# First half of the rows normalised, turned and multiplied in two quarters, with a new table of orders, in a float32 decoder block

## The chip, the cores and the metric

One core of a Trainium2 chip runs the whole kernel. The metric is the device time of one execution in microseconds (us), lower is better. Engines are named as the profile names them: PE multiplies, PEld loads its weights, DVE works elementwise, ACT does activations and casts, POOL is the second elementwise engine and also issues DMAs, SP issues DMAs only.

## The reference

```
h = rms_norm(x, norm_g)                          # x: 1024 rows x 1024
proj = h @ w_in                                  # u, g_rnn, q, k, v, g_attn, m_rnn, m_attn
u = causal_depthwise_conv(u)                     # width 4
y_rnn = rg_lru(u) * silu(g_rnn)                  # block-diagonal gates, linear recurrence over the rows
y_attn = sliding_window_attention_with_sinks(rope(q), rope(k), v) * silu(g_attn)   # 16 heads, 4 kv heads, window 128
merged = sigmoid(m_rnn) * (y_rnn @ w_rnn_out) + sigmoid(m_attn) * (y_attn @ w_attn_out)
out = rms_norm(x + merged @ w_o, final_norm_g)
```

All tensors are float32.

## The kernel before

**Products.** A float32 product is made of three matmuls: each operand is split into a high part (`h`, a cast by ACT) and a low part (`l`, what is left, a subtraction by DVE), and high·high, high·low and low·high are added up in PSUM. The wide projections run as *pairs* of output blocks: a pair and the two halves of the rows make a 2x2 block product, which `Pair.run` does with seven products instead of eight. Its right-hand operands are B11, B21, B22 and the combinations T1 to T4 of the transposed, normalised rows; its left-hand operands are the weight blocks A and their sums S1 to S4. Each is four tiles of 128x512 in two parts. B11 and B21 hold the first 512 rows, B12 and B22 the others.

**The opening.** Before any combination can exist, the rows have to come in. For each half of the rows (`hf`): the sum of squares of each block of 128 rows (`rstd_of`, on ACT or DVE), a scaling by DVE (L649 `xt<-xt,rs`), 32 transposes by PE (L656 `pt<-ident,xt`), and `cut_g`, which splits each of eight PSUM tiles into high (ACT, L438) and low (DVE, L439). So that PE has work meanwhile, two of the pairs that need no combination (`FIRST`, two output pairs of the merge gate) are multiplied plainly: `first_raw` loads their weights, `first_split` splits them into `dh` and `dl`, and `first_half(p, hf)` makes 2 outputs x 8 blocks x 3 matmuls of 512 columns (tile `fd`, L588 to L590). `F11` and `F21` keep the whole float32 rows of the first half for T1, T3 and T4; they are made by ACT again from PSUM (L673) or by POOL as the sum of both parts (L675).

**The order.** The program is recorded as a list of operations with costs, buffers and priorities (`Plan`), and a planner lays it out engine by engine. Each engine then runs its own list strictly in that order. What sets the list is the table `TUNE`: offsets to priorities (`prep`, `att`, `lru`, ...), limits of buffers by kind, and `orders`, the sequence of pairs (`ug`, `k`, `v`, `q`, `ga`, `ma`, `mr`, `zr`, `za`), of attention units (`a` with its key head and block) and of `s` entries. An `s` entry makes four sums ahead of time and parks them in DRAM: `s0` to `s7` of a pair's weights, `s8` to `s11` of `w_o`. The sums of `w_o` are read back only if `s8` is in the sequence, which it is in neither kernel.

Line numbers are those of the kernel before; in the changed one every line after the table stands 8 lower down, and those after the opening 36.

Of the kernel before, what the change touches and what calls it, by code (L numbers as in the profile page):

```python
# [17 lines left out]
S = 1024  # L18
D = 1024
P = 128  # L20
HF = 512
KT = D // P
# [38 lines left out]
    'val': 95,
    'gate': 951,
    'lru': -1407,
    'qk': -125,
    'comb': 348,
    'ztl': -10,
    'xof': 233,
    'gzr': 8,
    'gza': 42,
    'gwo': 14,  # L70
# [282 lines left out]
def hybrid_block_kernel(ctx: ExitStack, tc: tile.TileContext, x, wall, wo, bd, vec, gfin,  # L353
# [81 lines left out]
    def split(h, l, src, cols, reads, wh, wl, prio=0, psum=False, scale=None):  # L435

        if scale is not None:
            ACT(lambda e: e.activation(h(), src(), AF.Identity, scale=scale()), cols, reads, wh, prio, aps=1)  # L438
            DVE(lambda e: e.scalar_tensor_tensor(l(), src(), scale(), h().bitcast(F32), op0=MUL, op1=SUB), cols,  # L439
                list(reads) + list(wh), wl, prio, ptr=1)  # L440
            return
        ACT(lambda e: e.copy(h(), src()), cols, reads, wh, prio)  # L442
        (DVE if psum else EW)(lambda e: e.tensor_tensor(l(), src(), h().bitcast(F32), op=ALU.subtract), cols,  # L443
                              list(reads) + list(wh), wl, prio)
# [18 lines left out]
    def col(i):  # L463
        return vec_t.t[:, i : i + 1]
# [138 lines left out]
    HC["B12"] = [(buf("B12", dt=F32R, name="B12h"), buf("B12", dt=F32R, name="B12l")) for _ in range(4)]  # L603
    WD = {}

    def first_raw(p):
        for b, n in ((0, "A11"), (3, "A12"), (1, "A21"), (2, "A22")):
            raw = load("raw0", n)
            WD[p, n] = [raw]
            DMA(lambda raw=raw, b=b: raw.t, lambda b=b: wall[U_MR + p, b], 1 << 18, [], [raw])  # L610

    def first_split(p):
        for n in ("A11", "A12", "A21", "A22"):
            h, l = buf("wd", dt=F32R, name="dh"), buf("wd", dt=F32R, name="dl")
            split_buf(h, l, WD[p, n][0])
            WD[p, n] = (h, l)

    def first_half(p, hf):

        for q, names in enumerate((("A11", "A12"), ("A21", "A22"))):  # L620
            ps = bank("fd")
            for k in range(KT):
                h, l = WD[p, names[k // 4]]
                bh, bl = HC[("B11", "B21", "B12", "B22")[2 * hf + k // 4]][k % 4]
                w = slice(k % 4 * P, k % 4 * P + P)
                PE(lambda ps=ps, h=h, l=l, w=w, bh=bh, bl=bl, k=k: three(ps, h, l, w, bh, bl, k == 0, k == KT - 1), 3,
                   [h, l, bh, bl], [ps])
            gate_half("r", 2 * p + q, hf, ps)

    xs = []  # L630
    for s in range(NB):
        xs.append([slot("xt"), slot("xt")])
        for q in range(2):
            DMA(lambda s=s, q=q: xs[s][q].t, lambda s=s, q=q: x[s * P : (s + 1) * P, HALF[q]], 1 << 18, [], [xs[s][q]])
        if s == 0:
            DMA(lambda: vec_t.t, lambda: vec, 32768, [], [vec_t])
        if s == 3:
            first_raw(0)
    for p in FIRST[1:]:
        first_raw(p)  # L640
    F11, F21 = ([slot(n) for _ in range(4)] for n in ("F11", "F21"))
    for hf in range(2):
        pts = [bank("pt") for _ in range(KT)]
        for s4 in range(4):
            xh = xs[4 * hf + s4]
            rs = rstd_of(xh)
            for q in range(2):
                pl.op([("DVE", 395.0)], [xh[q], rs], [xh[q]], lambda e, q=q, xh=xh, rs=rs:
                      nc.vector.tensor_scalar(xh[q].t, xh[q].t, rs.t, None, op0=MUL), port=True)  # L649

        def cut_g(h, l, ps, k):
            split(lambda: h.t, lambda: l.t, lambda: ps.t, HF, [ps, vec_t], [h], [l], scale=lambda: col(V_G + k))

        def turn(s4, k, hf=hf, pts=pts):
            xh = xs[4 * hf + s4]
            PE(lambda: nc.tensor.transpose(  # L656
                pts[k].t[:, s4 * P : (s4 + 1) * P], xh[k // 4].t[:, (k % 4) * P : (k % 4 + 1) * P], ident),
               1, [xh[k // 4]], [pts[k]], 256)

        if hf == 0:  # L660
            for s4 in range(4):
                for k in range(KT):
                    turn(s4, k)
            for p in FIRST:
                first_split(p)
            for k in range(KT):
                h, l = HC["B11" if k < 4 else "B21"][k % 4]
                cut_g(h, l, pts[k], k)
                f = (F11 if k < 4 else F21)[k % 4]

                def whole(e, f=f, h=h, l=l, k=k, ps=pts[k]):
                    if e == "ACT":
                        nc.scalar.activation(f.t, ps.t, AF.Identity, scale=col(V_G + k))  # L673
                    else:
                        nc.gpsimd.tensor_tensor(f.t, h.t.bitcast(F32), l.t.bitcast(F32), op=ADD)  # L675
# [686 lines left out]
```

## Time and profile before

| | |
|---|---|
| median of 3 runs | 885.35 us (884.28 to 885.56) |
| the profiled execution, its own time | 885.57 us |
| its span in the trace | 883.8 us |
| busy: PE / DVE / ACT / POOL | 860.1 / 764.6 / 640.1 / 93.3 us |
| PE's first instruction | at 8.31 us |
| first product of the opening (`fd`) | at 17.78 us |
| first product on rows of the second half | at 48.41 us |

"Busy" is the time in which an engine has an instruction under way. The stages used below are the opening (0 to 48 us), the recurrent branch (48 to 315), attention (315 to 650), the two output projections (650 to 810), and the last projection with the final norm.

### The profile page before, as it was taken

How to read it: one execution, taken by the hardware profiler on the slowest of the kernel's cores; microseconds unless marked ns; L12 is line 12 of the kernel's file. 1: busy time of each engine (PE TensorE's matmuls, PEld its weight loads, DVE VectorE, ACT ScalarE, POOL GpSimd, SP SyncE). 2: the span in 40 equal slices, each digit the busy share in tenths (PEclk: the TensorE clock that was granted, in tenths of full speed). 3: DMA queues.
4: the chain of work that ended last, by engine and by line, in shares of the span. 5: the costliest groups of instructions: out<-in, count | busy, mean ns of one | idle time of the engine just before them, and what ended most of it. 6: DMA issues, size and time to landing. Idle time of an engine off the chain costs nothing.

```text
span 883.8 us, 13278 instructions
## 1 busy us (share of the span) xinstructions
PE 860.1 (97%) x4040; PEld 710.7 (80%) x4040; DVE 764.6 (87%) x1555; ACT 640.1 (72%) x1339; POOL 93.3 (11%) x161
## 2 busy tenths in 40 slices
PE   5899999999999999999999999999999999999996
PEld 4688877788878888888888888888888887888885
DVE  6998997889998888887887877868899999979968
ACT  7655758597986598988898899999884446343751
POOL 2101010100110011011001000001111121101030
PEclk9999999999999999999999999999999999999999
DMA  9538784611246745574843644444778898565155
GB/s 319 192 134 279 250 280 120 220 42 55 84 124 194 201 124 193 144 183 144 212 120 120 186 123 138 143 126 130 260 248 288 279 311 294 179 228 130 48 95 191
DMA packets 101000, 157.58 MB, mean 178 GB/s; under 512 B 12352, under 2 KB 41920, under 8 KB 100928
## 3 DMA queue, kind: packets, MB, share of 16 engines
q1 hardware_dynamic: 88160, 117.39, 41.4%
q0 software_dynamic: 12768, 39.33, 15.5%
q8 instruction: 32, 0.52, 0.3%
q14 instruction: 40, 0.33, 0.1%
HBM read 103.46 MB, written 53.22 MB: 177 GB/s over the span
## 4 chain that ended last, share of the span: by engine, by line
PE 58%; DVE 17%; ACT 6%; DMA 4%; issue 3%; DVEq 0%; SPq 0%; ACTq 0%
PE pair L531 15%; PE pair L532 15%; PE pair L533 15%; PE ps_s L922 3%; PE ptp L956 2%; DVE wl L443 2%; PE o L1233 2%; PE o L1232 2%; PE o L1231 2%; DVE c L450 1%; DVE S L450 1%; ACT sm L945 1%; PE po L969 1%; DVE cu L752 1%; PE po L970 1%
## 5 line engine op out<-in xcount | busy, mean ns | idle before, releaser
L428 POOL DMA_DIRECT2D A<-in_wall_dram x114 | 61.5, 540 | 591.1 <-PE pair L533 128.1
L442 ACT CAST wh<-S 128x512 fp32r<-128x512 f32 x128 | 78.4, 622 | 24.5 <-DVE S L450 18.9
L443 DVE TENSOR_TENSOR wl<-S,wh 128x512 fp32r<-128x512 f32 x128 | 87.1, 683 | 4.7 <-ACT wh L442 3.8
L443 DVE TENSOR_TENSOR wl<-A,wh 128x512 fp32r<-128x512 f32 x96 | 65.6, 684 | 10.0 <-ACT wh L442 9.7
L937 ACT ACTIVATE sm<-sm,nm 128x256 f32<-128x256 f32 (+1 forms) x128 | 62.2, 489 | 0.3 <-DVE nm L930 0.2
L442 ACT CAST wh<-A 128x512 fp32r<-128x512 f32 x96 | 59.4, 619 | 2.0 <-PE pair L533 1.0
L450 DVE TENSOR_TENSOR c<-pair,u 128x512 f32<-128x512 f32 x64 | 43.9, 686 | 17.4 <-ACT u L554 12.6
L930 DVE CUSTOM_DVE_ANT_0 sm<-ps_s,mask_t,sink_t 128x256 f32<-128x256 f32 (+1 forms) x128 | 53.9, 459 | 3.9 <-PE ps_s L922 3.8
L945 ACT ACTIVATE sm<-sm,dn 128x256 f32<-128x256 f32 (+1 forms) x128 | 53.6, 488 | 0.3 <-DVE dn L942 0.2
L531 PE MATMUL pair<-B11h,wh 128*128 128x512 f32 x128 | 51.6, 403 | 0.6 <-DVE B12l L439 0.6
L531 PE MATMUL pair<-T4h,wh 128*128 128x512 f32 x128 | 51.0, 398 | 0.5 <-ACT u L554 0.4
L531 PE MATMUL pair<-T1h,wh 128*128 128x512 f32 x128 | 51.3, 400 | 0.0
L531 PE MATMUL pair<-T2h,wh 128*128 128x512 f32 x128 | 51.2, 400 | 0.0
L531 PE MATMUL pair<-B21h,wh 128*128 128x512 f32 x128 | 51.1, 399 | 0.0
L531 PE MATMUL pair<-T3h,wh 128*128 128x512 f32 x128 | 50.4, 394 | 0.1
L532 PE MATMUL pair<-B22l,wh 128*128 128x512 f32 x128 | 49.9, 390 | 0.3 <-DVE B22l L443 0.3
L532 PE MATMUL pair<-T3l,wh 128*128 128x512 f32 x128 | 50.1, 391 | 0.1
L532 PE MATMUL pair<-T4l,wh 128*128 128x512 f32 x128 | 50.0, 391 | 0.1
L533 PE MATMUL pair<-B11h,wl 128*128 128x512 f32 x128 | 50.0, 391 | 0.0
L533 PE MATMUL pair<-T4h,wl 128*128 128x512 f32 x128 | 50.0, 390 | 0.0
L532 PE MATMUL pair<-B11l,wh 128*128 128x512 f32 x128 | 50.0, 390 | 0.0
L532 PE MATMUL pair<-T1l,wh 128*128 128x512 f32 x128 | 49.9, 390 | 0.0
(281 smaller groups left out, 2619.1 us busy)
## 6 DMA issues: line engine op xcount, KB each, us to landing
A<-in_wall_dram POOLq DMA_DIRECT2D x114, 256.0 KB, 3.4
qt<-st_q SPq DMA_DIRECT2D x32, 256.0 KB, 3.3
sr<-in_wall_dram SPq DMA_DIRECT2D x24, 256.0 KB, 4.6
sum<-S SPq DMA_DIRECT2D x24, 256.0 KB, 4.2
S<-sum POOLq DMA_DIRECT2D x24, 256.0 KB, 4.5
xt<-in_x_dram SPq DMA_DIRECT2D x16, 256.0 KB, 5.4
A<-in_wall_dram SPq DMA_DIRECT2D x16, 256.0 KB, 4.9
tm_r<-tm SPq DMA_DIRECT2D x16, 256.0 KB, 2.2
```

The source lines that it names most:

```text
L428: pl.op([("POOL", 1000.0)], reads, writes, lambda e: nc.gpsimd.dma_start(dst(), src()), prio, move=move)
L442: ACT(lambda e: e.copy(h(), src()), cols, reads, wh, prio)
L443: (DVE if psum else EW)(lambda e: e.tensor_tensor(l(), src(), h().bitcast(F32), op=ALU.subtract), cols, list(reads) + list(wh), wl, prio)
L450: (eng or EW)(lambda e: e.tensor_tensor(dst.t, a.t, b.t, op=op), HF, [a, b], [dst], prio)
L531: nc.tensor.matmul(ps.t, h.t[:, w], bh.t, start=start and k == 0, stop=False, **kw)
L532: nc.tensor.matmul(ps.t, h.t[:, w], bl.t, start=False, stop=False, **kw)
L533: nc.tensor.matmul(ps.t, l.t[:, w], bh.t, start=False, stop=k == 3, **kw)
L922: nc.tensor.matmul(ps.t[:, j, o0 : o0 + pw], qt.t[:, h, :], K[m, half].t[:, c0 : c0 + pw], start=m == 0, stop=m == 1)
L930: DVE(lambda v, ps=ps, j=j, h=h, s=s: v.tensor_tensor_reduce(s.t[:, j, :], ps.t[:, j, :], att["mask"].t[:, 256 - w : 256], scale=-0.125, s ...
L937: ACT(lambda e, h=h, s=s, j=j: e.activation(s.t[:, j, :], s.t[:, j, :], AF.Exp, scale=-1.0, bias=nm.t[:, h : h + 1], accum_out=dn.t[:, h : ...
L945: ACT(lambda e, h=h, s=s, j=j: e.activation(s.t[:, j, :], s.t[:, j, :], AF.Identity, scale=dn.t[:, h : h + 1]), w, [(s, j), dn], [(s, j)], ...
L956: PE(lambda pt=pt, h=h, b=b: nc.tensor.transpose(pt.t[:, h, :], sm[h // 2].t[:, h % 2, b * P : (b + 1) * P], ident), 1, [(sm[h // 2], h % ...
```

## The change

**Quarters.** For the first half of the rows, transposes, cuts and plain products are done in two quarters of 256 rows (`qq`): 16 transposes, eight cuts of 256 columns, then 96 matmuls of 256 columns per quarter. Two blocks `k` share a PSUM tile `pt`. Quarter 0 needs only the first two blocks of rows. The second half is done as before.

**F11 and F21** are no longer read from PSUM by ACT or added by POOL, but added from both parts after the second quarter (`EW`: DVE or POOL, as the planner puts it).

**Loads.** With `fwi` 2 the weights A11 and A12 of the first pair come ahead of row block 3, all others ahead of the second half of the rows.

**The table.** New numbers and another sequence of pairs, units and sums.

```diff
-    'S': 6,
+    'S': 4,
-    'B': 11,
+    'B': 13,
-    'prep': 270,
-    'att': 91,
+    'prep': 210,
+    'att': 117,
...
-    'orders': 'ug0 k0 ug7 v0 ug5 ug4 ug3 ug1 q0 q1 ug2 a00 ga0 ma2 a01 a02 a03 a10 a11 a04 a05 q3 a12 '
-              'a13 ga3 a14 q2 a15 s0 a06 s5 a07 s10 ug6 s3 ma1 mr3 a16 a20 a21 a17 s4 s6 a22 a23 a24 '
-              'ma0 ga2 a25 s1 a26 a30 a31 a32 a33 a34 ma3 a35 a36 a27 mr2 ga1 a37 zr0 zr1 zr2 zr3 za0 '
-              'za1 za2 za3',
+    'orders': 'ug0 ug3 k0 v0 ug5 s11 ug4 ug7 ug1 q0 q1 ug2 a00 s4 ma3 a01 a02 a03 a10 a11 ga2 a04 q3 '
+              'a12 a05 a13 ga1 ug6 a06 a14 s3 a15 s1 a07 q2 ga3 a16 ma2 a20 s9 a21 a22 a23 a17 a24 '
+              'mr3 a25 ma1 a30 a26 a31 a32 a33 a34 s0 a35 ma0 a36 a27 s5 ga0 mr2 a37 zr0 zr1 zr2 zr3 '
+              'za0 za1 za2 za3',
...
+    def first_quarter(p, qq):
+
+        for q, names in enumerate((("A11", "A12"), ("A21", "A22"))):
+            if qq == 0:
+                FD[p, q] = bank("fd")
+            ps = FD[p, q]
+            cs = slice(256 * qq, 256 * qq + 256)
+            for k in range(KT):
+                h, l = WD[p, names[k // 4]]
+                bh, bl = HC[("B11", "B21")[k // 4]][k % 4]
+
+                def go(ps=ps, h=h, l=l, w=slice(k % 4 * P, k % 4 * P + P), bh=bh, bl=bl, k=k):
+                    nc.tensor.matmul(ps.t[:, cs], h.t[:, w], bh.t[:, cs], start=k == 0, stop=False)
+                    nc.tensor.matmul(ps.t[:, cs], h.t[:, w], bl.t[:, cs], start=False, stop=False)
+                    nc.tensor.matmul(ps.t[:, cs], l.t[:, w], bh.t[:, cs], start=False, stop=k == KT - 1)
...
+            for qq in range(2):
                 for k in range(KT):
-                    turn(s4, k)
-            for p in FIRST:
-                first_split(p)
+                    for s4 in (2 * qq, 2 * qq + 1):
+                        xh, pt = xs[s4], pts[4 * qq + k // 2]
...
+                if qq == 0:
+                    first_split(0, 0)
+                for k in range(KT):
+                    h, l = HC["B11" if k < 4 else "B21"][k % 4]
+                    pt = pts[4 * qq + k // 2]
+                    cs = slice(256 * qq, 256 * qq + 256)
+                    split(lambda h=h, cs=cs: h.t[:, cs], lambda l=l, cs=cs: l.t[:, cs], lambda pt=pt, k=k: pt.t[:, k % 2, :], 256,
+                          [pt, vec_t], [(h, qq)], [(l, qq)], TUNE["cutp"], scale=lambda k=k: col(V_G + k))
+                if qq == 0:
+                    first_split(0, 1)
+                    for p in FIRST[1:]:
+                        first_split(p, 0)
+                        first_split(p, 1)
+                for p in FIRST:
+                    first_quarter(p, qq)
...
-                pl.op([("ACT", 569.0), ("POOL", 1245.0)], [h, l, pts[k], vec_t], [f], whole, port=True)
-            for p in FIRST:
-                first_half(p, 0)
+                EW(lambda e, f=f, h=h, l=l: e.tensor_tensor(f.t, h.t.bitcast(F32), l.t.bitcast(F32), op=ADD), HF, [h, l], [f])
```

**Where instructions went.** The program lists of both kernels, engine by engine, show it; a number after a name tells one buffer from another of the same name.

PE, around the first product, before: the last transposes of row block 3 (`xt_120`), then the first output `fd_321`.

```order
L656 MATMUL pt_196<-ident_69,xt_120 128x128
L656 MATMUL pt_198<-ident_69,xt_120 128x128
L656 MATMUL pt_202<-ident_69,xt_120 128x128
L588 MATMUL fd_321<-B11h_283,dh_206 128x512
L589 MATMUL fd_321<-B11l_295,dh_206 128x512
L590 MATMUL fd_321<-B11h_283,dl_231 128x512
```

PE, the same place now: `xt_104` and `xt_112` are row blocks 0 and 1, `xt_114` and `xt_116` block 2, `xt_122` block 3.

```order
L693 MATMUL pt_191<-ident_69,xt_112 128x128
L693 MATMUL pt_193<-ident_69,xt_112 128x128
L693 MATMUL pt_245<-ident_69,xt_114 128x128
L693 MATMUL pt_249<-ident_69,xt_114 128x128
L693 MATMUL pt_253<-ident_69,xt_116 128x128
L693 MATMUL pt_261<-ident_69,xt_116 128x128
L652 MATMUL fd_268<-B11h_227,dh_175 128x256
L653 MATMUL fd_268<-B11l_235,dh_175 128x256
L654 MATMUL fd_268<-B11h_227,dl_185 128x256
L652 MATMUL fd_268<-B11h_241,dh_175 128x256
L653 MATMUL fd_268<-B11l_259,dh_175 128x256
L654 MATMUL fd_268<-B11h_241,dl_185 128x256
```

The first product moved ahead of the transposes of row block 3; most of the second quarter's transposes now stand behind all 96 matmuls of the first.

DVE, between the first cuts, before (`dl` weights' low parts, L577 sums of squares of the second half's rows):

```order
L443 TENSOR_TENSOR dl_264<-A21_129,dh_253 128x512
L577 ISA junk_277,ss_260<-xt_144 128x512
L577 ISA ss_260 128x1
L443 TENSOR_TENSOR dl_286<-A22_135,dh_271 128x512
L439 SCALAR_TENSOR_TENSOR B11l_295<-pt_181,vec_t_106,B11h_283 128x512
L581 TENSOR_TENSOR ss_260<-ss_260 128x1
L577 ISA junk_302,ss_291<-xt_152 128x512
L577 ISA ss_291 128x1
L439 SCALAR_TENSOR_TENSOR B11l_311<-pt_183,vec_t_106,B11h_297 128x512
```

DVE, now, the first quarter's cuts (256 columns):

```order
L447 SCALAR_TENSOR_TENSOR B11l_235<-pt_180,vec_t_106,B11h_227 128x256
L451 TENSOR_TENSOR dl_243<-A21_129,dh_233 128x512
L592 RECIPROCAL rs_257<-sd_239 128x1
L447 SCALAR_TENSOR_TENSOR B11l_259<-pt_180,vec_t_106,B11h_241 128x256
L677 TENSOR_SCALAR xt_122<-xt_122,rs_257 128x512
L677 TENSOR_SCALAR xt_124<-xt_124,rs_257 128x512
L447 SCALAR_TENSOR_TENSOR B11l_275<-pt_182,vec_t_106,B11h_263 128x256
L447 SCALAR_TENSOR_TENSOR B11l_284<-pt_182,vec_t_106,B11h_277 128x256
L447 SCALAR_TENSOR_TENSOR B21l_291<-pt_191,vec_t_106,B21h_286 128x256
```

The first cut now stands ahead of the scaling of row block 3 and of four of the weights' low parts. From that cut to the first one of the second quarter DVE's list holds 8 cuts, 6 `dl`, one `wl`, three `S`, 10 scalings, 2 sums of squares and 15 tiny operations.

POOL, before, the sums that made five of the eight F tiles:

```order
L675 TENSOR_TENSOR F11_307<-B11h_283,B11l_295 128x512
L675 TENSOR_TENSOR F11_319<-B11h_297,B11l_311 128x512
L675 TENSOR_TENSOR F11_337<-B11h_313,B11l_327 128x512
L675 TENSOR_TENSOR F21_381<-B21h_353,B21l_367 128x512
L675 TENSOR_TENSOR F21_402<-B21h_385,B21l_393 128x512
```

DVE, now, behind the last S of the opening: the second quarter's last cuts, and all eight F tiles.

```order
L447 SCALAR_TENSOR_TENSOR B21l_331<-pt_261,vec_t_106,B21h_319 128x256
L715 TENSOR_TENSOR F11_540<-B11h_227,B11l_235 128x512
L715 TENSOR_TENSOR F11_545<-B11h_241,B11l_259 128x512
L715 TENSOR_TENSOR F11_553<-B11h_263,B11l_275 128x512
L715 TENSOR_TENSOR F11_561<-B11h_277,B11l_284 128x512
L715 TENSOR_TENSOR F21_568<-B21h_286,B21l_291 128x512
L715 TENSOR_TENSOR F21_577<-B21h_293,B21l_302 128x512
L715 TENSOR_TENSOR F21_585<-B21h_304,B21l_314 128x512
L715 TENSOR_TENSOR F21_592<-B21h_319,B21l_331 128x512
L447 SCALAR_TENSOR_TENSOR B12l_602<-pt_510,vec_t_106,B12h_527 128x512
L725 SCALAR_TENSOR_TENSOR T1_611<-pt_510,vec_t_106,F11_540 128x512
```

The F tiles left POOL and ACT, and DVE makes them between the second quarter and the first tile of the second half.

Over the whole program ACT's table loads go from 51 to 44, PE's matmuls from 4040 to 4136, the weights' parked sums from six sets to five, and the sets of `w_o` sums from one to two.

More of the change, by code (lines that the diff above doesn't have):

```diff
@@ L36 @@
     'pen': 99999,
-    'zy': 5,
-    'zg': 3,
+    'zy': 7,
+    'zg': 2,
     'raw': 4,
     'raws': 10,
-    'S': 6,
+    'S': 4,
     'wc': 11,
-    'B': 11,
-    'psw': 58,
+    'B': 13,
+    'psw': 82,
     'psk': 1,
@@ L47 @@
     'ld': 14,
-    'lds': 21,
+    'lds': 20,
     'kv': 8,
-    'kvs': 3,
+    'kvs': 0,
     'qt': 3,
-    'qts': 5,
-    'P': 16,
+    'qts': 3,
+    'P': 14,
     'AO': 22,
@@ L56 @@
     'xo': 24,
-    'lru0': -135,
-    'xos': 10,
-    'prep': 270,
-    'att': 91,
[L61 to L70, printed above, removed]
+    'lru0': -78,
+    'xos': 8,
+    'prep': 210,
+    'att': 117,
+    'val': 92,
+    'gate': 545,
+    'lru': -1714,
+    'qk': -43,
+    'comb': 775,
+    'ztl': -377,
+    'xof': 500,
+    'gzr': 9,
+    'gza': 38,
+    'gwo': 21,
     'gxo': 3,
@@ L75 @@
     'sil': 100,
+    'cutp': 0,
+    'fsp': 0,
+    'fwi': 2,
     'sump': 200,
@@ L83 @@
     'mgd': 1,
[4 rows of a table removed]
-}
[4 rows of a table added]
+}
+FW = ({1: [(0, 0)], 3: [(0, 1), (1, 0)], 5: [(1, 1)]}, {1: [(0, 0)], 2: [(0, 1)], 3: [(1, 0), (1, 1)]},
+      {2: [(0, 0)], 3: [(0, 1), (1, 0), (1, 1)]}, {3: [(0, 0)], 4: [(0, 1), (1, 0)], 5: [(1, 1)]},
+      {3: [(0, 0), (0, 1), (1, 0), (1, 1)]}, {1: [(0, 0)], 3: [(0, 1)], 4: [(1, 0)], 5: [(1, 1)]})
 V_CW, V_CB, V_BA, V_BX, V_LAM, V_G = 0, 32, 40, 48, 56, 64
@@ L604, in hybrid_block_kernel, with first_raw @@
     WD = {}
-    def first_raw(p):
-        for b, n in ((0, "A11"), (3, "A12"), (1, "A21"), (2, "A22")):
+    def first_raw(p, part):
+        for b, n in ((0, "A11"), (3, "A12"), (1, "A21"), (2, "A22"))[2 * part : 2 * part + 2]:
             raw = load("raw0", n)
@@ L610, in first_raw, with first_split @@
             DMA(lambda raw=raw, b=b: raw.t, lambda b=b: wall[U_MR + p, b], 1 << 18, [], [raw])
-    def first_split(p):
-        for n in ("A11", "A12", "A21", "A22"):
+    def first_split(p, part):
+        for n in (("A11", "A12"), ("A21", "A22"))[part]:
             h, l = buf("wd", dt=F32R, name="dh"), buf("wd", dt=F32R, name="dl")
-            split_buf(h, l, WD[p, n][0])
+            split_buf(h, l, WD[p, n][0], TUNE["fsp"])
             WD[p, n] = (h, l)
@@ L628, in first_half @@
             gate_half("r", 2 * p + q, hf, ps)
+    FD = {}
+    def first_quarter(p, qq):
[11 more added lines that the diff above has]
+                    nc.tensor.matmul(ps.t[:, cs], l.t[:, w], bh.t[:, cs], start=False, stop=k == KT - 1)
+                PE(go, 3, [h, l, (bh, qq), (bl, qq)], [ps], 256)
+            if qq:
+                gate_half("r", 2 * p + q, 0, ps)
     xs = []
@@ L636, in hybrid_block_kernel @@
             DMA(lambda: vec_t.t, lambda: vec, 32768, [], [vec_t])
[L637 to L640, printed above, removed]
+        for p, part in FW[TUNE["fwi"]].get(s, ()):
+            first_raw(p, part)
     F11, F21 = ([slot(n) for _ in range(4)] for n in ("F11", "F21"))
     for hf in range(2):
-        pts = [bank("pt") for _ in range(KT)]
+        pts = [bank("pt") for _ in range(KT)] if hf else [bank("pt", [P, 2, 256]) for _ in range(KT)]
         for s4 in range(4):
@@ L660, in hybrid_block_kernel @@
         if hf == 0:
-            for s4 in range(4):
+            for qq in range(2):
                 for k in range(KT):
-                    turn(s4, k)
-            for p in FIRST:
-                first_split(p)
+                    for s4 in (2 * qq, 2 * qq + 1):
+                        xh, pt = xs[s4], pts[4 * qq + k // 2]
+                        PE(lambda s4=s4, k=k, xh=xh, pt=pt: nc.tensor.transpose(
+                            pt.t[:, k % 2, (s4 % 2) * P : (s4 % 2 + 1) * P], xh[k // 4].t[:, (k % 4) * P : (k % 4 + 1) * P], ident),
+                           1, [xh[k // 4]], [pt], 256)
+                if qq == 0:
[13 more added lines that the diff above has]
+                    first_quarter(p, qq)
             for k in range(KT):
                 h, l = HC["B11" if k < 4 else "B21"][k % 4]
-                cut_g(h, l, pts[k], k)
+                pl.op([("SP", 0)], [(h, 0), (h, 1), (l, 0), (l, 1)], [h, l], lambda e: None)
                 f = (F11 if k < 4 else F21)[k % 4]
[L671 to L675, printed above, removed]
-                pl.op([("ACT", 569.0), ("POOL", 1245.0)], [h, l, pts[k], vec_t], [f], whole, port=True)
-            for p in FIRST:
-                first_half(p, 0)
+                EW(lambda e, f=f, h=h, l=l: e.tensor_tensor(f.t, h.t.bitcast(F32), l.t.bitcast(F32), op=ADD), HF, [h, l], [f])
         else:
```

## The prediction

> **What bounds the kernel now.** The page first: busy time of the engines, and the chain of work that ended last.
>
> ```profile
> PE 860.1 (97%) x4040; PEld 710.7 (80%) x4040; DVE 764.6 (87%) x1555; ACT 640.1 (72%) x1339; POOL 93.3 (11%) x161
> ...
> PE 58%; DVE 17%; ACT 6%; DMA 4%; issue 3%; DVEq 0%; SPq 0%; ACTq 0%
> ```
>
> PE is busy for 97% of the span and carries 58% of the chain. Where its idle 23.7 us lie, the table by stage says (stretch, its length, then busy us of PE, PEld, DVE, ACT, POOL):
>
> ```profile
> 0.00:48.00 48.00, 34.45 (x162) 28.07 (x163) 38.98 (x109) 35.05 (x75) 8.42 (x11) 1.00 0.76 262
> 48.00:315.00 267.00, 265.84 (x1173) 217.55 (x1172) 243.03 (x401) 188.13 (x312) 23.85 (x44) 1.00 0.51 162
> 315.00:650.00 335.00, 334.49 (x1718) 281.00 (x1718) 271.10 (x685) 303.31 (x736) 30.64 (x57) 1.00 0.55 163
> 650.00:810.00 160.00, 159.61 (x705) 130.63 (x704) 149.08 (x245) 77.41 (x147) 22.53 (x40) 1.00 0.74 246
> 810.00:853.00 43.00, 42.88 (x189) 34.89 (x188) 40.24 (x67) 28.79 (x56) 6.78 (x8) 1.00 0.37 73
> 853.00:884.00 31.00, 22.79 (x101) 18.55 (x99) 22.20 (x53) 7.38 (x21) 1.08 (x2) 0.94 0.48 154
> ```
>
> 13.55 us lie in the opening and 8.2 in the final norm's tail. Between 48 and 853 us, the whole of pairs and attention, PE idles 1.16 + 0.51 + 0.39 + 0.12 = 2.2 us. So a new order of pairs can win about 2 us at most; it can lose more. The opening is the place to look, in PE's waits and then in its timeline (start, length, instruction, idle time before it):
>
> ```profile
> PE pt L656 <- DVE xt L649: 9.0, 2, 8.3
> PE fd L588 <- DVE B11l L439: 1.5, 1, 1.5
> PE fd L589 <- DVE B21l L439: 1.2, 1, 1.2
> PE fd L589 <- DVE B11l L439: 1.2, 1, 1.2
> PE pair L531 <- DVE B12l L439: 0.6, 1, 0.6
> ```
>
> ```profile
> 8.31 3.65 PE L656 MATMUL pt<-ident,xt 128*128 128x128 f32 x16 [8.31 <-DVE xt L649]
> 12.65 3.68 PE L656 MATMUL pt<-ident,xt 128*128 128x128 f32 x16 [0.69 <-DVE xt L649]
> 17.78 0.50 PE L588 MATMUL fd<-B11h,dh 128*128 128x512 f32 x1 [1.45 <-DVE B11l L439]
> ...
> 42.95 0.39 PE L589 MATMUL fd<-B21l,dh 128*128 128x512 f32 x1
> 43.18 0.40 PE L590 MATMUL fd<-B21h,dl 128*128 128x512 f32 x1
> 43.42 3.65 PE L656 MATMUL pt<-ident,xt 128*128 128x128 f32 x32
> 47.66 0.47 PE L531 MATMUL pair<-B11h,wh 128*128 128x512 f32 x1 [0.58 <-DVE B12l L439]
> ```
>
> Every wait names DVE. Matmuls of 512 columns start 0.227 us apart (42.95 to 43.18 is one step), so the 96 of the first half are 21.8 us of work; they took 17.78 to 43.42, that is 25.6. The mark for the sum is 47.66 us: there all of the first half is multiplied, the 32 transposes of the second are done, and PE idles next to nothing for 800 us.
>
> **The change, part by part.** Prices of the new forms, from the nearest rows. A matmul of 256 columns and a DVE cut of 256 columns both stand elsewhere in this trace:
>
> ```profile
> 336.62 1.12 PE L922 MATMUL ps_s<-K,qt 128*128 128x256 f32 x8
> 337.61 0.48 PE L922 MATMUL ps_s<-K,qt 128*128 128x256 f32 x2
> ...
> 160.94 2.07 DVE L439 SCALAR_TENSOR_TENSOR vst<-pv,vst 128x256 fp32r<-128x256 f32 x6
> ...
> L438 ACT ACTIVATE vst<-pv 128x256 fp32r<-128x256 f32 x8 | 2.5, 387 | 2.4 <-PE pv L866 2.2
> ...
> L439 DVE SCALAR_TENSOR_TENSOR vst<-pv,vst 128x256 fp32r<-128x256 f32 x8 | 2.8, 412 | 0.0
> ```
>
> Eight such matmuls take 337.61 - 336.62 = 0.99 us, 0.124 each, so a quarter's 96 take 11.9 and both 23.8, 2.0 more than before. A DVE cut lasts 0.41 us and repeats every (2.07 - 0.41) / 5 = 0.33; one of ACT lasts 0.39.
>
> *Start.* What ACT does before its first cut stays nearly the same: seven sums of squares, two casts of weights, three roots. Before, this ended with the second cast:
>
> ```profile
> 12.49 0.60 ACT L442 CAST dh<-A 128x512 fp32r<-128x512 f32 x1
> 13.11 1.28 ACT L716 ACT_TABLE_LOAD   x1
> ```
>
> So the first cut can start at 13.1 us; with 0.39 on ACT and 0.41 on DVE the first product comes at about 14.0, 3.8 us earlier than 17.78. The table load and two casts that stood ahead of it are moved behind it.
>
> *The first quarter.* PE's own work is 11.9 us plus 14 transposes, which at full pace (3.65 us for 32) are 1.6: it could be through at 27.5. DVE can't feed the second quarter by then. From its first cut at 13.5 to the second quarter's, its list (in the order) has 8 cuts x 0.33, 10 subtractions or sums, 10 scalings, 2 sums of squares and 15 tiny operations. Their repeat times:
>
> ```profile
> 56.59 1.89 DVE L450 TENSOR_TENSOR T<-T,F 128x512 f32<-128x512 f32 x3
> ...
> 33.30 2.45 DVE L649 TENSOR_SCALAR xt<-xt,rs 128x512 f32<-128x512 f32 x6
> ...
> L577 DVE CUSTOM_DVE_ANT_0 junk<-xt 128x512 f32<-128x512 f32 x4 | 2.7, 686 | 1.0 <-DMA xt<-in_x_dram 1.0
> ```
>
> That is 0.60, 0.40 and 0.69, and 0.1 for a tiny one: 2.6 + 6.0 + 4.0 + 1.4 + 1.5 = 15.5 us, so 29.0 is the floor. I take 31.0, because ACT and DVE also hand PSUM tiles to and fro, as here, where ACT waited until DVE had read the same tile:
>
> ```profile
> 23.95 0.69 ACT L673 ACTIVATE F<-pt,vec_t 128x512 f32<-128x512 f32 x1 [1.34 <-DVE B11l L439]
> ```
>
> In the first quarter two cuts share a tile, eight such turns; a quarter of a microsecond each is my estimate. The second quarter's first product then comes at 31.3. PE's 3 us of spare time ahead of it cost nothing, because DVE would not let it go on earlier.
>
> *The second quarter and the mark.* Its cuts come every 0.36 to 0.39 us, its products use up 0.37 per cut and output and there are four outputs, so PE runs through: 31.3 + 11.9 = 43.2. Four of the second half's transposes are already done; 28 more are 3.2 us, five of them between products. PE is at the mark at 46.4, against 47.66: **1.2 us won**. The ends: with DVE at its floor 29.0 it is 3.2; with DVE 2 us later than I take it, a loss of 0.8.
>
> *F tiles.* DVE gets 8 x 0.60 = 4.8 us. It loses what POOL's sums did to it; while they ran, tiny DVE operations of 0.16 us took up to 1.28:
>
> ```profile
> 17.80 4.75 POOL L675 TENSOR_TENSOR F<-B11h,B11l 128x512 f32<-128x512 f32 x3 [16.49 <-DVE ss L581]
> ...
> 21.43 1.16 DVE L726 TENSOR_SCALAR ab<-vec_t 128x8 f32<-128x8 f32 x1
> ...
> 27.73 1.28 DVE L723 TENSOR_TENSOR acc<-acc,z 128x8 f32<-128x8 f32 x1
> ```
>
> The cover for the rest is DVE's lead. Before, its last T1 part started here:
>
> ```profile
> 69.23 0.68 DVE L443 TENSOR_TENSOR T1l<-T,T1h 128x512 fp32r<-128x512 f32 x1
> ```
>
> PE needs it after 117 matmuls from the mark (96 plain ones, 12 of A11 x B11, 9 of T1): 47.66 + 26.6 = 74.2, a lead of 4.3 us. After: second cuts to 34.2, F to 39.0, then by the order ten larger operations (6.7 us with the tiny ones between), 14 of 0.66 and 24 of 0.60 to about 69.8; PE needs it at 46.4 + 26.6 = 73.0. The lead is 3.2 and holds. Cost nothing; without that lead up to 4.8.
>
> *Loads.* The second half's rows go behind four more weights on SP, 4 x 256 KB; at 390 GB/s in this stretch that is 2.7 us.
>
> ```profile
> 10.00:15.00 5.00, 4.31 (x21) 3.90 (x20) 3.38 (x11) 4.97 (x13) 0.00 (x0) 1.00 1.05 396
> 15.00:20.00 5.00, 3.41 (x15) 2.35 (x14) 4.97 (x13) 5.00 (x14) 2.19 (x2) 1.00 1.05 386
> ...
> 15.02 0.63 ACT L575 ACTIVATE junk<-xt 128x512 f32<-128x512 f32 x1
> ```
>
> ACT squared the first of these rows at 15.0 before, so it lands by 17.7 now; by the order ACT asks for it seven cuts and two casts after 13.1, at 17.0 or, with the turns, 18.7. Hidden, or late by 0.7 on an engine that waits for DVE there.
>
> *The rest of the table.* One more set of dead `w_o` sums and one pair whose S are made in place: DVE +4 x 0.60 = 2.4 us, covered by its 24 idle us between 48 and 315; POOL's queue gets three loads fewer. ACT drops seven table loads of 1.28, 9 us, and in attention it is busy 303.3 of 335, so some of PE's 2.2 us should go; I take 1.0, with ends of 2.2 won and 2.2 lost (its idle time doubled). The tail has the same list on PE; nothing there.
>
> **Sum.** 1.2 + 1.0 = 2.2 us: span 881.6, own time 885.57 - 2.2 = 883.4, and since the profiled execution is 0.2 above the median, 883.2 on the runs' scale. 0.2% or 1.8 us is about what a measurement here can tell from no change.
>
> **Rivals.** *(a) No change:* the opening's gain is given back, because DVE is late with a T tile or the second half's cuts. For it: DVE's 4.97 of 5.00 us in the row from 15 to 20. Against: the 3.2 us of lead. If the 1.2 goes, 884.4; with the 1.0 too, 885.4.
>
> *(b) The array stays at half pace in the thin first quarter: slower.* The first 32 transposes took 3.65 us per 16, the later ones 3.65 for 32, though the granted clock reads 1.00 in both stretches. If PE, fed now in drops, stays at half pace over all 96 products, they take 23.8 instead of 11.9 us: 14.0 + 23.8 + 1.6 + 0.9 for the cuts = 40.3 instead of 31.3, so 9 us later than in the sum: 892. Its 3 us of spare time hide the first 24 half-paced products at 0.124 each; beyond 42 the whole gain is gone, beyond 56 it is measurably slower. Against it: at 17.78, after 1.45 us idle, products ran at once at full pace.
> The Trainium skill (TensorE: Matmul & The Clock Gate, The HAM clock gate) says the array starts at half clock and gets the full one after about 3.4 us of sustained activity, in a window that runs freely. By an estimate from that page, with PE fed steadily from 15.4 us, at most some 30 products are half-paced, 6 beyond what is hidden: 0.7 us, 883.9 instead of 883.2. The half pace agrees with the trace; the granted clock in it does not show it.
>
> *(c) Weight loads set the pace of short matmuls.* PEld's 710.7 us over 4040 are 0.176 each, more than 0.124; then the second quarter takes 5.0 us longer, 888.2. Against: the L922 rows, one load each, ran at 0.124.
>
> *(d) The new order stalls in the middle: slower.* A pair whose weights or combinations come late stops PE for 0.6 us, as the last of the waits above did. With the opening's 1.2 kept, five such stops make 885.35 - 1.2 + 3.0 = 887.2, the point from which it is measurably slower; seven make 888.4. Against: 2.2 us in all 800 now, with the same limits of work per engine; for it: 15 of 32 pairs change places.
>
> **Chances.** The sum, with opening and middle near the values taken, 0.50 (0.40 of it faster, 0.10 same); opening at DVE's floor, 880 to 882, 0.17; (a) 0.18; (b) 0.05; (c) 0.03; (d) 0.07, all three slower. Faster 0.57, same 0.28, slower 0.15. The low end is 885.35 - 3.2 - 2.2 = 880.0; the high end takes in (a) and half of (d), 886.5.
>
> **What would show it.** Right: first `fd` near 14, second quarter's first near 31, the mark near 46.4, POOL without sums, PE idle under 2.2 us from the mark to 853. Wrong: products 0.2 us apart in the first quarter (b, c); DVE idle before B11l, waiting for ACT (my two microseconds too small); PE waits on T tiles between 60 and 80 us (a), or on `u`, `c`, `pw` behind 100 (d).

## The result, and the profile after

The changed kernel takes 891.74 us (median of 6 runs, 889.87 to 893.17), the kernel before 885.45 us in runs beside it (6 runs, 884.28 to 886.91). The ratio is 1.007 with a 95% interval of 1.0056 to 1.0085: **slower by 0.7%**, where 883.2 us was forecast. The profiled execution took 891.28 us, its span is 889.5 us. From the page of the changed kernel, busy time and the chain that ended last:

```profile
PE 862.8 (97%) x4136; PEld 717.1 (81%) x4136; DVE 768.7 (86%) x1573; ACT 634.5 (71%) x1339; POOL 83.7 (9%) x153
...
PE 67%; DVE 15%; ACT 9%; DMA 4%; issue 4%; SPq 1%; DVEq 0%; ACTq 0%
```

PE's busy time grew by 2.7 us, ACT's and POOL's fell, and PE still sets the time. The changed kernel's table by stage (stretch, length, busy us of PE, PEld, DVE, ACT, POOL, then granted clock, DMA share, GB/s) says where PE is idle now:

```profile
0.00:48.00 48.00, 35.77 (x262) 34.26 (x263) 38.95 (x106) 33.47 (x80) 0.70 (x6) 0.96 0.69 242
48.00:315.00 267.00, 266.08 (x1184) 218.23 (x1183) 245.95 (x428) 190.30 (x313) 23.80 (x44) 1.00 0.54 167
315.00:650.00 335.00, 330.96 (x1678) 276.73 (x1677) 264.97 (x661) 292.89 (x718) 30.52 (x57) 0.99 0.54 157
650.00:810.00 160.00, 158.48 (x704) 129.22 (x703) 151.72 (x256) 79.29 (x150) 19.13 (x35) 1.00 0.74 253
810.00:853.00 43.00, 43.00 (x191) 35.42 (x191) 42.93 (x72) 29.20 (x56) 6.08 (x7) 1.00 0.27 45
```

From 48 to 853 us PE idles 0.92 + 4.04 + 1.52 + 0 = 6.5 us, three times the 2.2 of before, and in the attention stage the granted clock is no longer 1.00. PE's waits in the changed kernel name the places:

```profile
PE pt L693 <- DVE xt L677: 8.7, 1, 8.7
PE ps_s L958 <- DMA K<-st_k: 2.6, 1, 2.6
...
PE pair L540 <- DVE T3l L451: 1.2, 2, 1.1
...
PE pair L539 <- ACT u L555: 1.0, 2, 0.7
```

The second row is new: in all of the kernel before PE never waited for K. PE's timeline there and in the opening:

```profile
8.72 4.57 PE L693 MATMUL pt<-ident,xt 128*128 128x128 f32 x20 [8.72 <-DVE xt L677]
14.53 0.39 PE L652 MATMUL fd<-B11h,dh 128*128 128x256 f32 x1 [1.24 <-DVE B11l L447]
...
16.83 0.55 PE L652 MATMUL fd<-B11h,dh 128*128 128x256 f32 x1 [1.11 <-DVE B11l L447]
...
31.91 0.36 PE L652 MATMUL fd<-B11h,dh 128*128 128x256 f32 x1
...
43.51 2.89 PE L684 MATMUL pt<-ident,xt 128*128 128x128 f32 x25
46.15 0.48 PE L596 MATMUL fd<-B12h,dh 128*128 128x512 f32 x1
...
354.98 0.22 PE L958 MATMUL ps_s<-K,qt 128*128 128x128 f32 x1
357.80 3.40 PE L958 MATMUL ps_s<-K,qt 128*128 128x128 f32 x15 [2.60 <-DMA K<-st_k]
```

The opening went as forecast: first product at 14.53, the second quarter's first at 31.9, its last just ahead of 43.5. At 46.15 three of the 64 transposes are still to come, so the mark (first half multiplied, second half transposed) is 46.15 + 3 x 0.11 = 46.5. The last two rows are the loss: PE stands for 2.6 us, and then 15 small matmuls take 3.40 us, 0.21 each, where the same form ran at 0.11. The granted clock says why (same columns as above, stretches of the opening and of the stop):

```profile
16.60:20.00 3.40, 3.17 (x15) 3.20 (x16) 2.83 (x7) 2.89 (x8) 0.00 (x0) 0.50 1.05 387
...
354.50:357.90 3.40, 0.80 (x5) 0.51 (x4) 2.89 (x5) 2.71 (x5) 0.54 (x1) 1.00 0.97 224
357.90:361.30 3.40, 3.40 (x16) 3.40 (x17) 2.47 (x13) 3.11 (x12) 0.00 (x0) 0.51 1.06 376
```

Behind the stop the array ran at half clock for 3.4 us. Stop and half pace together cost some 4.4 us: the excess of PE's start-to-start times over full pace, summed over 340 to 400 us, is 7.4 us against 3.0 before. SP's timeline in the changed kernel shows who was late:

```profile
347.15 0.32 SPq L434 DMA_DIRECT2D yr_dr<-tg  x1
348.15 0.32 SPq L434 DMA_DIRECT2D sg_dr<-tga  x1
350.60 0.32 SPq L434 DMA_DIRECT2D yr_dr<-tg  x1
351.01 2.46 SPq L434 DMA_DIRECT2D K<-st_k  x4
```

The four loads of key head 1's last two K tiles need nothing that was late, but SP issues in the order of its list, and there they stand behind two stores of `tg`. The second `tg` product is the last step of DVE's chain for the recurrence (DVE's timeline):

```profile
348.56 1.28 DVE L821 TENSOR_TENSOR_SCAN hs<-r,hs,i 128x512 f32<-128x512 f32 x1
349.88 0.69 DVE L458 TENSOR_TENSOR tg<-tg,hs 128x512 f32<-128x512 f32 x1
```

### The profile page after: what moved, and what is told of

Its sections match the earlier page's. It is cut to its first block, busy times and chain, and to the rows that moved or that the text cites. A ratio compares the mean times of both kernels' runs of the same rounds, so it can differ in the third digit from the quotient of the medians.

```text
span 889.5 us, 13510 instructions
## 1 busy us (share of the span) xinstructions
PE 862.8 (97%) x4136; PEld 717.1 (81%) x4136; DVE 768.7 (86%) x1573; ACT 634.5 (71%) x1339; POOL 83.7 (9%) x153
## 4 chain that ended last, share of the span: by engine, by line
PE 67%; DVE 15%; ACT 9%; DMA 4%; issue 4%; SPq 1%; DVEq 0%; ACTq 0%
PE pair L539 16%; PE pair L540 16%; PE pair L541 16%; PE ps_s L958 2%; PE o L1269 2%; PE o L1268 2%; PE o L1267 2%; DVE wl L451 2%; ACT sm L973 2%; ACT sm L981 2%; PE ptp L992 2%; DVE c L458 1%; DVE S L458 1%; DVE cu L788 1%; DVE hs L821 1%
## 5 line engine op out<-in xcount | busy, mean ns | idle before, releaser
L539 PE MATMUL pair<-B22h,wh 128*128 128x512 f32 x128 | 50.0, 391 | 0.3 <-DVE c L458 0.3
L540 PE MATMUL pair<-B21l,wh 128*128 128x512 f32 x128 | 50.1, 392 | 0.1
L541 PE MATMUL pair<-T2h,wl 128*128 128x512 f32 x128 | 50.0, 391 | 0.0
L541 PE MATMUL pair<-T3h,wl 128*128 128x512 f32 x128 | 50.0, 391 | 0.0
```

Of the source, the lines that this page charges most:

```text
L539: nc.tensor.matmul(ps.t, h.t[:, w], bh.t, start=start and k == 0, stop=False, **kw)
L540: nc.tensor.matmul(ps.t, h.t[:, w], bl.t, start=False, stop=False, **kw)
L541: nc.tensor.matmul(ps.t, l.t[:, w], bh.t, start=False, stop=k == 3, **kw)
```

## The experiments

The theory: the new table (numbers and order of pairs) made the loss, as single stops of PE, the one for K first. The rivals: the quarters themselves made the later stages late (F tiles on DVE); or the loss is no sum of places but PE's normal state under another list. Each group of runs had the kernel before beside it; it took 885.55, 886.16 and 885.52 us there.

| run | median, us | ratio to before (95%) |
|---|---|---|
| the change | 891.74 | 1.0070 (1.0056 to 1.0085) |
| quarters_oldtable | 886.73 | 1.0020 (1.0008 to 1.0032) |
| halves_newtable | 890.00 | 1.0061 (1.0049 to 1.0073) |
| k_first | 888.91 | 1.0046 (1.0034 to 1.0058) |
| quarters_oldorders | 900.43 | 1.0174 (1.0159 to 1.0188) |
| quarters_oldnumbers | 903.78 | 1.0202 (1.0182 to 1.0222) |
| filled_pause | 894.41 | 1.0098 (1.0083 to 1.0113) |
| filled_at_355 | 890.99 | 1.0058 (1.0045 to 1.0072) |
| k_first_tz | 886.07 | 1.0001 (0.9991 to 1.0011) |
| quarters_oldtable_fix | 887.52 | 1.0013 (1.0003 to 1.0024) |
| mended | 886.34 | 1.0010 (1.0001 to 1.0019) |

**The change in two halves.** In *quarters_oldtable* the code is the changed one and the table that of before; in *halves_newtable* the code is that of before and the table the new one.

```diff
 # quarters_oldtable, against the changed kernel (all numbers of the table, and the orders)
-    'S': 4,
+    'S': 6,
...
-    'orders': 'ug0 ug3 k0 v0 ug5 s11 ...
+    'orders': 'ug0 k0 ug7 v0 ug5 ug4 ...
 # halves_newtable, against the kernel before: the same lines the other way round
```

> The changed kernel's quarters, F tiles and order of loads with the kernel before's table (its numbers and its order of pairs and units). If the opening did its work and the new table is the loss (theory), the opening's 1.2 us stays: 884.2 on the runs' scale (883 to 885.4), first quarter's first product near 14, the mark near 46.4, and no stop of over 2 us in the middle. If the quarters themselves make the middle late (rival: F tiles on DVE, DVE behind in the first units), it stays slow: 889 to 892. A third way: the planner lays out everything anew from the first changed operation, so a stall of its own of 1 to 3 us can turn up anywhere, 885 to 888.

> The kernel before's opening (halves, F sums on ACT and POOL) with the changed table. If the table is the loss (theory): slower than before by what the middle lost, 5 to 7 us, so 891 to 893, with PE stopped for 2 us or more by K loads behind yr_dr stores in SP's queue near 355, and half-paced products behind it. If the quarters are the loss (rival): as before, 884 to 887.

The new table alone costs 4.5 us, a little less than the 5 to 7 that were expected. The stages of halves_newtable from 48 to 810 us:

```profile
48.00:315.00 267.00, 264.15 (x1171) 217.01 (x1170) 241.89 (x399) 188.06 (x309) 23.81 (x44) 1.00 0.53 161
315.00:650.00 335.00, 332.73 (x1701) 278.24 (x1700) 268.10 (x674) 296.07 (x725) 30.52 (x57) 1.00 0.55 159
650.00:810.00 160.00, 158.50 (x702) 129.28 (x701) 151.71 (x256) 78.57 (x148) 19.13 (x35) 1.00 0.75 252
```

PE idles 2.85 + 2.27 + 1.50 = 6.6 us, as much as in the changed kernel, with the old opening. The granted clock stays at 1.00. Most of the idle time is the changed kernel's other stops and new ones:

```profile
PE pv L863 <- DVE c L447: 1.4, 1, 1.4
PE pair L529 <- DVE T3l L440: 1.2, 2, 1.1
...
PE pair L528 <- ACT u L551: 1.1, 2, 0.9
```

The stop for K is there, but it is only 0.7 us, so the expected 2 us were wrong (SP's timeline, then PE's):

```profile
353.05 2.44 SPq L423 DMA_DIRECT2D K<-st_k  x4
```

```profile
357.00 0.22 PE L919 MATMUL ps_s<-K,qt 128*128 128x128 f32 x1
357.95 1.97 PE L919 MATMUL ps_s<-K,qt 128*128 128x128 f32 x15 [0.73 <-DMA K<-st_k]
```

SP issues the loads behind the same stores as in the change, and in both kernels PE comes to the unit 4.0 us after the first issue (353.05 to 357.00 here, 351.01 to 354.98 there). Here PE goes on 4.9 us after the issue, in the change 6.8. So the list makes the place, and the time that the loads take to land sets its price. Why they landed later in the change is open.

The quarters alone are 1.2 us slower, not 1.2 faster: the third way of the expectation, a stall of their own. The longest stop behind their opening is new (PE's waits of quarters_oldtable):

```profile
PE pv L899 <- DVE c L455: 1.8, 1, 1.8
```

DVE's list held `c<-pair,u` behind a whole recurrence, and that behind two sums which waited 4.7 us for a weight load (DVE's timeline):

```profile
156.05 0.69 DVE L455 TENSOR_TENSOR S<-A,A 128x512 f32<-128x512 f32 x1 [4.72 <-DMA A<-in_wall_dram]
...
164.14 0.68 DVE L455 TENSOR_TENSOR c<-pair,u 128x512 f32<-128x512 f32 x1
```

The table is the same as in the kernel before, but the planner lays out everything behind the first changed operation anew, and so this order of DVE's is not that of before.

**Numbers or order.** *quarters_oldorders* takes the sequence of before with the new numbers, *quarters_oldnumbers* the new sequence with the numbers of before.

> The changed kernel with its table's numbers, but the kernel before's order of pairs and units. If the order of units is what puts key head 1's loads behind the stores (theory in its first form), the stop at 355 goes and the time is 884 to 887. If the numbers do it (kvs from 3 to 0, lru from -1407 to -1714, which say when loads and the LRU's steps may go), the stop stays or moves: 888 to 893.

> The changed kernel with the kernel before's numbers, but its own new order of pairs and units. If the order makes the stops by key head 1's K loads at 355 and by u at 470 (theory), both are there and the stops near 738 are not: 888 to 890. If the numbers make them all (rival): 885 to 887.

Both are far slower than either whole table, by 15 and 18 us against before. In quarters_oldorders one stop does it:

```profile
PE o L1265 <- DVE T2l L448: 11.3, 1, 11.3
```

In quarters_oldnumbers it is a dozen stops, the largest near 439 and from 606 to 622 us; no stop for K. So the table works as a whole, and these runs do not say which of its two parts made the loss: both expectations missed. The clock fell twice in quarters_oldnumbers, once behind a pause of 2.10 us at 439 us, and once behind two pauses of 1.47 and 0.22 us just ahead of 609 us. The longest pause, 2.38 us, had no half clock behind it (stretches as above, then PE's timeline):

```profile
609.03:612.44 3.41, 2.86 (x11) 1.80 (x9) 0.59 (x2) 3.39 (x11) 0.54 (x1) 0.50 0.45 115
612.44:615.85 3.41, 1.58 (x10) 1.32 (x11) 3.41 (x13) 3.38 (x11) 0.00 (x0) 1.00 0.21 38
```

```profile
614.27 0.33 PE L992 MATMUL ptp<-ident,sm 128*128 128x128 f32 x1 [2.38 <-ACT sm L981]
```

**The K loads.** *k_first* moves one thing in the list that the planner made: the four DMAs stand ahead of the `yr_dr` and `sg_dr` stores.

```diff
...
-        for _, i, e in self.run():
+        seq = [(i, e) for _, i, e in self.run()]
+        k1 = [x for x in seq if self.ops[x[0]]["lab"] == "kv1" and self.ops[x[0]]["bufs"][0].name == "K"][4:]
+        to = max(p for p, (i, e) in enumerate(seq[: seq.index(k1[0])]) if e == "SP" and self.ops[i]["bufs"][0].name == "tm") + 1
+        rest = [x for x in seq[to:] if x not in k1]
+        for i, e in seq[:to] + k1 + rest:
...
```

> The changed kernel, but the four DMAs of the last two K tiles of key head 1 go ahead of the two yr_dr stores and the sg_dr store in SP's queue; nothing else moves on another engine. If the stop of 2.6 us at 355 is the queue's and the 3.41 us of half-paced array behind it follow from the stop (theory), both go: PE no longer waits for K, the products at 358 run at 0.11, and the time falls by 3.5 to 4.5 us, to 887.2 to 888.2. If the half pace comes by itself (rival: it belongs to the time and not to the pause), it falls by 2.6 at most, to 889.1. If another wait stands right behind K (qt or DVE's softmax of the unit before), it falls by less than 1: 890.8 or more.

2.8 us less than the change, where 3.5 to 4.5 had been expected; 888.91 lies nearer to the 889.1 of the rival, by which the half pace comes without the stop. The trace decides between them. SP of k_first issues the loads 9 us earlier, and PE runs through (SP's timeline, then PE's):

```profile
342.04 2.42 SPq L439 DMA_DIRECT2D K<-st_k  x4
348.57 0.33 SPq L439 DMA_DIRECT2D yr_dr<-tg  x1
```

```profile
356.33 2.02 PE L963 MATMUL ps_s<-K,qt 128*128 128x128 f32 x16
```

Sixteen matmuls in 2.0 us against 0.22 + 2.6 + 3.40 in the change: stop and half pace both went. The excess from 340 to 400 us fell from 7.4 to 3.7, so 3.7 were won at the place and 0.8 lost again in this execution from 700 to 750.

**Does the pause make the half pace?** *filled_at_355* leaves K as late as it is and gives PE work that nothing reads. *filled_pause* was to do the same, with 11 products of 512 columns, and had them at the wrong unit, (1, 4, 0).

```diff
                 def go(ps=ps, j=j, h=2 * hp2 + j):
+                    for _ in range(20 if (g, n, h) == (1, 0, 0) else 0):
+                        nc.tensor.matmul(ps.t.rearrange("p a b -> p (a b)"), qt.t[:, 0, :],
+                                         qt.t[:, 0:2, :].rearrange("p a b -> p (a b)"), start=True, stop=True)
                     for half, c0, o0 in pieces:
```

> The changed kernel with 11 products of 512 columns that nothing reads, put on PE right ahead of the unit that waits for K at 355 (11 x 0.227 = 2.5 us of work inside the 2.6 us pause); SP's queue and all other work stay, so K lands as late as before. If the half pace behind the stop is made by the array's idleness (theory), the clock record of 0.5 from 358 to 361.4 goes, the 15 products behind run at 0.11 instead of 0.21, and the time falls by 1.4 to 1.7 us against the changed kernel, to about 890.1, while the wait for K still ends near 357.8. If the half pace comes from elsewhere (rival), the record stays and the time is 891.7 to 892.0.

> The changed kernel with 20 products of 256 columns that nothing reads (20 x 0.12 = 2.4 us), now right ahead of the unit that waits for K at 355, inside its pause of 2.6 us; the K loads land as late as before. (The run before this one had put its filling ahead of key head 1's fifth unit, at 423, where PE does not wait, so it told nothing of the pause and cost the 2.5 us that its products take.) If the half pace behind the stop comes of the array's idleness (theory): no record of 0.5 near 358, the 15 products there at 0.11, 1.4 to 1.7 us less than the changed kernel's 891.7, so 890.0 to 890.3. If not (rival): the record stays, 891.7 to 892.2.

PE of filled_at_355:

```profile
354.70 2.56 PE L957 MATMUL ps_s<-qt 128*128 128x256 f32 x20
357.09 0.22 PE L961 MATMUL ps_s<-K,qt 128*128 128x128 f32 x1
357.69 1.97 PE L961 MATMUL ps_s<-K,qt 128*128 128x128 f32 x15 [0.38 <-DMA K<-st_k]
```

K comes at 357.7, as in the change, and the 15 matmuls take 1.97 us instead of 3.40: idleness makes the half pace. The three profiles of the change's list without this filling (both of the change, and filled_pause) all have half clock behind the stop, this one has none. The run is 0.8 us under the change by its median, 1.1 by the ratios; 1.4 to 1.7 had been expected. The two intervals overlap, so the time alone shows no gain. The misplaced filling cost 2.7 us by its median, 2.5 by the ratios, which is what its products take, and its profile gave one more pause (PE of filled_pause):

```profile
358.03 2.17 PE L961 MATMUL ps_s<-K,qt 128*128 128x128 f32 x15 [2.12 <-DMA K<-st_k]
360.00 0.63 PE L539 MATMUL pair<-T1h,wh 128*128 128x512 f32 x1
```

Here the pause is 2.1 us, the 15 matmuls take 2.17 us, and the half pace comes only behind them (0.63 us instead of 0.39 for a matmul of 512 columns).

**The stops near 738 us.** *k_first_tz* adds to k_first that three of DVE's operations near 718 us go ahead of a `tz` product.

```diff
+        for a, b in [(4151, 4113), (4249, 4113), (4267, 4113)]:
+            x = next(q for q in seq if q[0] == a)
+            seq.remove(x)
+            seq.insert(next(p for p, q in enumerate(seq) if q[0] == b), x)
...
```

> The kernel with the K loads first (888.9 us), and three of DVE's operations near 718 (c from pair and c, the S part wl, the first T2l) go ahead of the tz product that waits 2.75 us for its load there. If DVE's list is what makes T3l late at 736 to 738 and the three stops there (1.25, 0.3, 0.3 us) are that idle time come due (theory), they shrink to under 0.5 together and the time falls by 1.2 to 1.8 us, to 887.1 to 887.7. If T3l is late because DVE has too much to do from 719 to 738 whatever the order (rival), or PE just stops later, the time stays at 888.5 to 889.

DVE in k_first, and then in k_first_tz:

```profile
718.66 0.69 DVE L1100 SCALAR_TENSOR_TENSOR tz<-tz,c 128x512 f32<-128x512 f32 x1 [2.75 <-DMA tz<-tm_r]
```

```profile
715.76 0.69 DVE L463 TENSOR_TENSOR T2l<-T,T2h 128x512 fp32r<-128x512 f32 x1
716.88 0.69 DVE L1107 SCALAR_TENSOR_TENSOR tz<-tz,c 128x512 f32<-128x512 f32 x1 [0.42 <-DMA tz<-tm_r]
```

The three operations fill the wait, and PE's wait for T3l fell from 1.2 to 0.5 us, 20 us further on:

```profile
PE pair L552 <- DVE T3l L463: 0.5, 2, 0.3
```

From 700 to 750 us the excess fell by 2.1 us; by the medians the run is 2.8 us under k_first, by the ratios 4.0, against an expected 1.2 to 1.8. What was won beyond the 2.1 is not explained by the moved operations. With two lists mended, the changed kernel is level with the kernel before.

**Two more mends.** *quarters_oldtable_fix* mends DVE's list at 155 us, *mended* adds three moves to k_first_tz.

```diff
 # quarters_oldtable_fix: c ahead of the second scan, the two S sums behind the recurrence's first steps
+        for a, b in [(791, 733), (946, 791), (953, 791)]:
 # mended: the three moves of k_first_tz, then tz behind two T2l, c ahead of tg at 350, two po steps (with what reads them) at 468
+        for a, b in [(4151, 4113), (4249, 4113), (4267, 4113), (4186, 4293), (1908, 1572), (2528, 2676), (2529, 2676)]:
```

> The quarters with the kernel before's table (886.7 us), and in DVE's list near 155 the LRU's first steps go ahead of two S sums that wait 4.7 us for a weight load, and c from pair and u goes ahead of the second scan. If the stop of 1.83 us at 163 is where the opening's 1.2 us went (theory), it falls to 0.5 or less, and the time by 1.3 to 1.8 us, to 885.0 to 885.4: equal to the kernel before, or just under it. If the quarters cost time by something else (rival), it stays at 886.2 or more.

> k_first_tz (886.1) with three more mends of the lists: the next tz product that waits for its load (1.15 us of DVE at 721) goes behind two T2l, c from pair and u goes ahead of the tg product at 350, and two po steps fill PE's stop of 0.84 us for u at 468. If the table's loss is the sum of single stops, each a matter of one list (theory), the stops at 350, 468 and 733 fall by 0.3, 0.8 and 0.3 and the time is 884.6 to 885.0 on that batch's scale, 1 us under the kernel before. If PE is then held by the next thing in line (rival), 886.0 as it was.

Neither won anything, where 1.3 to 1.8 us and 1 us had been expected. In the first the stop at 163 us is gone, so DVE's order had made it, and one that quarters_oldtable did not show stands at 135.2 (PE's waits of quarters_oldtable_fix):

```profile
PE psb L805 <- ACT uh L454: 1.0, 1, 1.0
```

It lies ahead of the moved operations, where both kernels run the same list, so two executions of one list can differ by a stop of this size; what made it is open. In *mended* the stops at 468 and 733 us shrank as wanted, and PE waited elsewhere, the longest at 482 us (0.78, for `c`). That fits the rival: what a small stop gives back, the next in line takes. It is not shown, because this profile also has two stops, 0.54 and 0.56 us, at 94 and 127 us, ahead of everything that was moved, and k_first_tz has neither. No version beat the kernel before.

**How steady the places are.** Both kernels ran once more for a second profile.

> The kernel before, once more, for a second profile of it: how far its first product's start (8.31 us in the first profile) and its stops move between executions. If the later first products of the kernels run since (8.1 to 9.6) are the noise of the first loads, this one lies in that range too, and its opening from first product to mark is again 39.3 us; its stops are the same within 0.2 us.

> The changed kernel, once more, for a second profile: if the stop for K at 355 is made by the order of the lists (theory), it is there again with 2.2 to 2.9 us and the array at half pace for 3.41 us behind it; if it was an accident of one execution, it is under 1 us. From first product to mark it takes 37.7 us again.

They took 885.36 and 894.25 us. The stop for K is there again, and larger (PE, then the clock, in after_again):

```profile
355.51 0.22 PE L958 MATMUL ps_s<-K,qt 128*128 128x128 f32 x1
359.20 3.54 PE L958 MATMUL ps_s<-K,qt 128*128 128x128 f32 x15 [3.46 <-DMA K<-st_k]
```

```profile
359.00:365.90 6.90, 6.70 (x23) 6.01 (x24) 5.43 (x24) 4.44 (x17) 0.54 (x1) 0.51 0.95 300
```

SP had issued the loads at 351.54, again 4.0 us ahead of PE, and PE went on 7.7 us after the issue. 3.5 us of stop and 6.8 us of half clock: the spread of the changed kernel's runs, 3.3 us, is of the size of this place's own. before_again starts PE's first transpose at 9.49 instead of 8.31 us and has its mark at 47.38 instead of 47.66, so the time from there to the mark is not the constant that was expected (37.9 us against 39.3). From the first `fd` product, which waits for DVE's `B11l`, it is 29.8 and 29.9 us: that product's start goes with the mark, and an early first transpose gains nothing.

## Why the prediction was wrong, by its own steps

- **The opening, 1.2 us won: right in kind, 0.7 in size.** First product, second quarter and last product came within 0.7 us of the forecast. Marks in three executions with halves: 47.66, 47.38 and 47.02, mean 47.35; in eleven with quarters 46.20 to 47.14, mean 46.64. The forecast had taken the 47.66 of a single execution for the kernel.
- **Half pace in the thin first quarter (rival b): there, and small.** 14 products of the first quarter ran at 0.21 us each, 9 to 25 in the other ten executions. In the six that show a granted clock of 0.50 in the opening, as above, the mark is at 46.86 on average, in the other five at 46.38. So the executions with 13 to 25 such products are half a microsecond later than those with 9 to 11. The Trainium skill (TensorE: Matmul & The Clock Gate, The HAM clock gate) had let me estimate 0.7 us; the traces agree with it that far. How the half pace gets into the mark is not shown, because in the change PE still waits 1.2 us for `B11l` ahead of the second quarter; the 3 us of spare time were too many.
- **F tiles and loads, nothing:** held. No PE wait on T tiles between 60 and 80 us in either profile of the change.
- **The middle, 1.0 us won, ends 2.2 either way: the step that failed.** It took PE's idle time for something that follows from the engines' sums of work: ACT has less to do, so some of the idle time goes. ACT did get 5.6 us freer, and PE's idle time rose from 2.2 to 6.5 us, with 1.4 us of half clock on top (15 matmuls in 3.40 instead of 1.97 us). The two stops that experiments traced come from positions in single lists: four DMAs behind a store, one product ahead of the load it needs. The far end, "its idle time doubled", had no row behind it.
- **The new order stalls in the middle (rival d): what happened,** and it was given 0.07. Its price was taken from a stop of 0.6 us, which it called one for a pair's weights or combinations; the row names `B12l`, a part of the rows at the end of the opening. The largest stop was 2.6 to 3.5 us, on a DMA queue the prediction never looked at, and it carries a second price, the half clock behind it, that no stop in the middle of the kernel before was long enough to show.
- **What is shown, and what is open.** Table by itself +4.5 us, quarters by themselves +1.2, both +6.3. That this is close to a sum is partly chance, because the stop for K costs 0.7 us with the table alone and some 4.4 with both. k_first and k_first_tz together take back 6.2 of the 6.3 (886.07 beside 886.16), so these two places carry most of the loss. They are not all of it: summed over 48 to 853 us, the excess over full pace is about 20 us in the kernel before, 27 in the change and still 22 in k_first_tz, whose earlier mark (46.4 against 47.7 us) makes up for part of the rest. Where the quarters with the old table lose their 1.2 us is open: the stop at 163 us went when DVE's operations were moved, and the time did not fall.

## What to carry to other kernels

When a change re-lays a schedule, forecast it from the lists and not from busy sums: on every queue, look for a load that stands behind a store whose data come late, and price it by the time from its issue to its use against the time that it takes to land (4.0 us against 4.9 to 7.7 here). A kernel whose PE idles 2 us in 800 has far more to lose by a new order than to win. A pause of PE of some 2 us can have a second cost behind it, the half clock, and in these traces mostly had it. One profile is not enough for a figure of half a microsecond.

## What the hardware showed that I had not expected

- Half clock comes after much shorter pauses than I thought, and in steps of 3.4 us: after 2.60 us idle one such step, after 3.46 us two, after 2.12 us one that began 1.6 us after PE had gone on, after 1.83 us (quarters_oldtable) none. The length of one pause does not decide it: two pauses of 1.47 and 0.22 us had a step behind them, as had the two of 1.24 and 1.11 us in the opening of the change, and one of 2.38 us had none. What decides it is open. The Trainium skill (TensorE: Matmul & The Clock Gate, The HAM clock gate) says that the clock falls after at least one idle window of about 3.4 us, and that windows run freely; the step's length agrees, the needed idleness does not: pauses of 2.1 us, and less in pieces, were enough here.
- 20 matmuls that nobody reads, put into the pause, let the 15 behind them run in 1.97 us instead of 3.40. The kernel's median was 0.8 us lower, which is not clear of the noise.
